# A hybrid decoder layer on one core: the two token mixers run half by half, 192 instead of 160 tokens take the gathered path, and the one-hots become float32

## The chip, the cores and the metric

The kernel runs on one core of a Trainium2 chip. TensorE multiplies matrices, VectorE (DVE in the profile) and ScalarE (ACT) work on tiles elementwise, GpSimd (POOL) here only issues the gathers of expert rows, and SyncE (SP) issues most of the other transfers. The metric is the device time of one execution in microseconds, lower being better. Before the change it is 3966.98 us, the median of three runs (3959.84 to 3968.33).

## What is computed

One decoder layer for 512 tokens of width 2048, with a final norm. Two mixers read the same normed input: HGRN2, a gated linear recurrence over chunks of 64 tokens with 8 heads, and latent attention (MLA) with 8 heads. Gates merge them, an output projection follows. Then comes PEER, a channel mixer in which each token picks 8 x 16 of 16384 single-neuron experts, and a gated per-layer embedding.

```python
proj = rms_norm(x, norm_mix) @ w_in
hq, hf, hi, hog, mq, mkv, mkr, ga, gb = split(proj)
o_a = hgrn2_branch(hq, hf, hi, hog, lb, hg_norm)      # S_t = diag(exp(g_t)) S_{t-1} + k_t v_t^T
o_b = mla_branch(mq, mkv, mkr, positions, ...)        # causal attention
y = sigmoid(ga) * (o_a @ w_a) + sigmoid(gb) * (o_b @ w_b)
x = x + y @ w_o
x = x + peer_ffn(rms_norm(x, norm_ffn), peer_wq, k1, k2, u, v)
x = x + sigmoid(rms_norm(x, norm_ple) @ w_pg) * (p @ w_pe)
return rms_norm(x, norm_final)
# peer_ffn, per token and head: q = h @ wq; top 16 of 128 keys in each half, top 16 of
# their 256 sums; gate = softmax; z = u[e] . h; out = sum(gate * gelu(z) * v[e])
```

## The kernel before

**Products.** A float32 product is made of three passes on values split in two: `hi` is the rounded value, `lo` the rest, and `mm3` (L151 to L153) adds `hi*hi`, `hi*lo` and `lo*hi`. Weights arrive in tiles of 128x2048 (1 MB) as two transfers into the ring `raw` (four halves); `Stream.split` makes `hi` on ScalarE (L115) and `lo` on VectorE (L116), into rings of four halves each. A tile is used in 48 matmuls, with all tokens of the stage as the moving columns (`cols_proj`) or with the weights as moving columns and blocks of 128 tokens as the fixed side (`rows_proj`, L181 to L183).

**Stages.** First the mixers for all 512 tokens: HGRN2 in two groups of four heads (projections, then per head exponentials, products, seven chunk states and the readout), then the latents, the rotary key and attention in four pairs of heads. Between the heads of attention run the gate projections of tokens 0 to 255 (`gate_proj`). Up to here, and for merge, output projection and PEER scores of tokens 0 to 255, the compiler's planner orders the instructions. Then `manual_schedule` begins: from here each engine works in the order in which the program is written. Tokens 256 to 511 go through their 32 gate projections, merge, output projection and scores. Then come U and V: in U (128 steps of 48 matmuls) every expert's `u` is multiplied with the tokens of the dense path, in V (128 steps of 48 matmuls) the activations are multiplied with every expert's `v`. A tail with the embedding gate and the output follows.

**Two paths of PEER.** The first NA + NX = 160 tokens don't take the dense path: their experts' rows are gathered. One gather brings 128 rows of 2048 values, one per partition; a `row_op` on VectorE multiplies it with `hrow` (u, L915) or adds it to `hrow` with a coefficient (v, L924), and calls the next gather (L904). Three row buffers are in flight. Tokens 0 to 127 need 128 gathers for u and 128 for v; the 32 tokens of NX lie four times side by side and need 32 and 32: 320 `row_op` in all. The other ND = 352 tokens are dense. For each, `gate_tokens` builds two one-hot tiles (L997 to L1003), multiplies them (L1008) so that its gates land on a 128x128 grid of experts, and stores that grid to DRAM (`G_s`), from which V reads it (`act_load`).

**Work beside.** `background()` runs once per weight tile in the manual part and takes topk (`prep_A` for tokens 0 to 127, `prep_B(b)` for block b) and `row_op` from the list `todo` by steps. In U, `work` holds `prep_B(2)`, `prep_B(3)` and `gate_tokens`, and `row_op` is spread evenly; in V too (VROWS = 148). Before U there are NEARLY = 36 `row_op`.

Of the kernel before, what the change touches and what calls it, by code (L numbers as in the profile page):

```python
# [20 lines left out]
T = 512  # L21
# [4 lines left out]
NX = 32  # L26
# [24 lines left out]
def kernel(ctx: ExitStack, tc: tile.TileContext, a, dbg=None):  # L51
# [44 lines left out]

    class Stream:
# [158 lines left out]
    def load_constants():  # L256
        m = t2()[:, :384]
        nc.sync.dma_start(m, a["masks"])
        nc.sync.dma_start(cst, a["consts"])
        V.tensor_copy(masks, m)  # L260
        V.tensor_copy(tril, m[:, 128:256])

# [13 lines left out]
    xpool = tc.alloc_tile_pool(name="xpool", bufs=1, side="right")  # L276
    xh = xpool.tile([128, KT, T], F32R, name="xh")
    xl = xpool.tile([128, KT, T], F32R, name="xl")

    def x_chunk(k):  # L280
        r = t2()
        nc.sync.dma_start(r, a["xT"][k])
        split(xh[:, k], xl[:, k], r, g_mix[:, k:k + 1])

    xblocks = [(xh[:, :, b * 128:(b + 1) * 128], xl[:, :, b * 128:(b + 1) * 128]) for b in range(4)]

    hg = tc.alloc_tile_pool(name="hg", bufs=1, side="left")
    masks = hg.tile([128, 384], F32R, name="masks")
    tril = hg.tile([128, 128], U32, name="tril")

    ss = tmp.tile([128, 4], F32, name="ss", bufs=1)
    ss2 = tmp.tile([128, 2, 4], F32, name="ss2", bufs=1)

# [11 lines left out]


# [15 lines left out]
    abuf = []  # L322
    for i in range(2):
        t = hg.tile([128, 4, 128], F32, name=f"abuf{i}")
        G.memset(t, 0.0)
        abuf.append(t)

    def first_chunks(i):
        x_chunk(2 * i)
        x_chunk(2 * i + 1)  # L330
        if i == 1:
            load_constants()

    rc_mix = rr_mix = None
    for hh in range(2):
        cs = slice(hh * 512, (hh + 1) * 512)
        ps_f = rows_proj([a["w_f"][hh, q] for q in range(4)], xblocks,
                         None if hh else first_chunks)
        if hh == 0:
            rc_mix, rr_mix = x_stats()  # L340
        lb, omlb = lower_bound(cs)
        gh = hg.tile([128, 4, 512], F32R, name="gh")
        gl = hg.tile([128, 4, 512], F32R, name="gl")
        k_t = hg.tile([128, 4, 512], F32, name="k_t")
        v_t = hg.tile([128, 4, 512], F32, name="v_t")
        qT = hg.tile([128, 4, T], F32, name="qT")
        ogT = hg.tile([128, 4, T], F32, name="ogT")
        for b in range(4):
            f = t2()
            S.activation(f, ps_f[b], AF.Sigmoid, scale=rc_mix[:, b:b + 1])  # L350
            V.tensor_tensor(f, f, omlb, op=OP.mult)
            V.tensor_tensor(f, f, lb, op=OP.add)
            V.tensor_scalar(k_t[:, b], f, -1.0, 1.0, op0=OP.mult, op1=OP.add)
            S.activation(f, f, AF.Ln)
            split(gh[:, b], gl[:, b], f)
            if hh == 0:
                dump(f"g_t{b}", f)
        ps_i = rows_proj([a["w_i"][hh, q] for q in range(4)], xblocks)
        for b in range(4):
            S.activation(v_t[:, b], ps_i[b], AF.Copy, scale=rc_mix[:, b:b + 1])  # L360
        for c in range(4):
            ps = cols_proj(a["w_q"][hh * 4 + c], xh, xl)
            V.tensor_tensor(qT[:, c], ps, rr_mix, op=OP.mult)
        for c in range(4):
            ps = cols_proj(a["w_og"][hh * 4 + c], xh, xl)
            V.tensor_tensor(ogT[:, c], ps, rr_mix, op=OP.mult)
            S.activation(ogT[:, c], ogT[:, c], AF.Silu)
        if hh == 0:
            dump("v_t", v_t)
            dump("qT", qT)  # L370
            dump("ogT", ogT)

        kTs = []
        for h in range(4):
            hs = slice(h * 128, (h + 1) * 128)
            kT_ps = mx()
            for b in range(4):
                TE.transpose(kT_ps[:, b * 128:(b + 1) * 128], k_t[:, b, hs], ident)
            kT = hg.tile([128, T], F32, name="kT", bufs=4)
            S.activation(kT, kT_ps, AF.Copy)  # L380
            kTs.append(kT)
        for b in range(4):
            dps = mx()
            TE.matmul(dps, lhsT=masks[:, 256:], rhs=gh[:, b], start=True, stop=False)
            TE.matmul(dps, lhsT=masks[:, 256:], rhs=gl[:, b], start=False, stop=True)
            e4 = t2()
            S.activation(e4, dps, AF.Exp)
            V.tensor_tensor(k_t[:, b], k_t[:, b], e4, op=OP.mult)

        for h in range(4):  # L390
            head = hh * 4 + h
            hs = slice(h * 128, (h + 1) * 128)
            e1 = hg.tile([128, 4, 128], F32, name="e1", bufs=2)
            e3 = hg.tile([128, 4, 128], F32, name="e3", bufs=1)
            qe = hg.tile([128, T], F32, name="qe", bufs=1)
            e2 = hg.tile([128, 4, 128], F32, name="e2", bufs=1)
            for bb in range(2):
                bps = mx().rearrange("p (b m t) -> p b m t", b=2, m=2)
                for b in range(2):
                    TE.matmul(bps[:, b], lhsT=gh[:, bb * 2 + b, hs], rhs=masks[:, :256], start=True, stop=False)  # L400
                    TE.matmul(bps[:, b], lhsT=gl[:, bb * 2 + b, hs], rhs=masks[:, :256], start=False, stop=True)
                o = slice(bb * 2, bb * 2 + 2)
                S.activation(e1[:, o], bps[:, :, 0], AF.Exp)
                S.activation(e2[:, o], bps[:, :, 0], AF.Exp, scale=-1.0)
                S.activation(e3[:, o], bps[:, :, 1], AF.Exp)
            qin, kin, eb = flat(e1), flat(e2), flat(e3)
            V.tensor_tensor(qin, qin, qT[:, h], op=OP.mult)
            V.tensor_tensor(kin, kin, kTs[h], op=OP.mult)
            V.tensor_tensor(qe, eb, qT[:, h], op=OP.mult)
            A_ps = mx()  # L410
            for b in range(4):
                bs = slice(b * 128, (b + 1) * 128)
                TE.matmul(A_ps[:, bs], lhsT=kin[:, bs], rhs=qin[:, bs], start=True, stop=True)
            ab = abuf[head % 2]
            for b in range(4):
                V.copy_predicated(ab[:, b], tril, A_ps[:, b * 128:(b + 1) * 128])
            states = [None]
            for n in range(7):
                dS = mx()
                r = slice((n % 2) * 64, (n % 2) * 64 + 64)  # L420
                TE.matmul(dS[:, :128], lhsT=k_t[r, n // 2, hs], rhs=v_t[r, n // 2, hs],
                          start=True, stop=True)
                st = hg.tile([128, 128], F32, name="st", bufs=8)
                if n == 0:
                    S.activation(st, dS[:, :128], AF.Copy)
                else:
                    V.scalar_tensor_tensor(st, states[-1], eb[:, n * 64 + 63:n * 64 + 64], dS[:, :128],
                                           op0=OP.mult, op1=OP.add)
                states.append(st)
            o_ps = mx()  # L430
            for b in range(4):
                bs = slice(b * 128, (b + 1) * 128)
                TE.matmul(o_ps[:, bs], lhsT=v_t[:, b, hs], rhs=ab[:, b], start=True, stop=False,
                          skip_group_check=True)
                for n in (2 * b, 2 * b + 1):
                    if n:
                        ns = slice(n * 64, n * 64 + 64)
                        TE.matmul(o_ps[:, ns], lhsT=states[n], rhs=qe[:, ns], start=False,
                                  stop=n == 2 * b + 1, skip_group_check=True)
# [6 lines left out]
        for h in range(4):  # L446
# [4 lines left out]
            dump(f"oa{head}", kTs[h])  # L451
    hg.release()

    def gate_proj(src, dst):
        w = Stream(src)
# [1060 lines left out]
```

## Time and profile before

| | |
|---|---|
| median of three runs | 3966.98 us |
| profiled execution, its own time | 3957.45 us |
| its span | 3955.7 us |
| TensorE busy | 3873.2 us, 98% |
| VectorE busy | 2950.8 us, 75% |
| ScalarE busy | 1750.3 us, 44% |
| GpSimd busy | 496.4 us, 13% |
| moved | 1011.64 MB, mean 256 GB/s |
| granted TensorE clock, mean share | 0.993 |

Busy time says how long an engine had an instruction in it. Matmuls are pipelined, so the time that one costs is the distance from its start to the next one's start, which is shorter than its own duration. The stages by time from the start of the span: mixers and gates of tokens 0 to 255 until 889.4 us, merge to scores of tokens 0 to 255 until 1178.1, gates of tokens 256 to 511 until 1375.1, their merge to scores until 1725.8, U until 2764.6, V until 3758.5, tail until 3955.7.

### The profile page before, as it was taken

The numbers are of one execution on the slowest core, as the hardware profiler recorded it, in microseconds if no ns is written. First come the engines' busy times: TensorE is split into PE (matmuls) and PEld (weight loads), VectorE is DVE, ScalarE is ACT, GpSimd is POOL, SyncE is SP. The second block draws the span as 40 slices with busy tenths as digits, with TensorE's granted clock in tenths as the row PEclk, the third lists the DMA queues.
The fourth block names the chain that finished last, engine by engine and source line by source line (L and its number), as shares of the span: only waits on it lengthen the run. The fifth ranks groups of instructions, "written<-read, shape, count | busy, mean of one in ns | idle before, by whom it ended". The sixth has DMA issues, their size and how long they took to land. (4 is left out here: it accounts for less than half of the span.)

```text
span 3955.7 us, 63576 instructions
## 1 busy us (share of the span) xinstructions
PE 3873.2 (98%) x24825; PEld 3677.9 (93%) x24825; DVE 2950.8 (75%) x4439; ACT 1750.3 (44%) x2814; POOL 496.4 (13%) x326
## 2 busy tenths in 40 slices
PE   9999999999999999899999999999999999999998
PEld 7878788899999989899999999999999999999987
DVE  5252555557658798789989898886888989899854
ACT  5242434345544434455555466663333333333443
POOL 0000000000000111012222222221122222222000
PEclk9999999999999999999999999999999999999999
DMA  5222234457766988788888888989999999899533
GB/s 212 96 75 96 70 99 134 130 184 238 231 203 205 330 280 299 268 293 314 317 319 301 306 324 308 338 310 357 359 346 346 368 356 353 330 360 361 195 120 99
DMA packets 312875, 1011.64 MB, mean 256 GB/s; under 512 B 29952, under 2 KB 127744, under 8 KB 269696
## 3 DMA queue, kind: packets, MB, share of 16 engines
q1 hardware_dynamic: 224032, 595.02, 44.1%
q0 software_dynamic: 46080, 335.56, 22.3%
q10 hardware_dynamic: 42464, 77.00, 5.1%
q8 instruction: 196, 3.21, 0.3%
q14 instruction: 103, 0.84, 0.1%
HBM read 931.18 MB, written 76.28 MB: 255 GB/s over the span
## 5 line engine op out<-in xcount | busy, mean ns | idle before, releaser
L116 DVE TENSOR_TENSOR lo<-raw,hi 128x1024 fp32r<-128x1024 f32 x966 | 1163.7, 1221 | 599.2 <-ACT hi L115 590.7
L115 ACT ACTIVATE hi<-raw 128x1024 fp32r<-128x1024 f32 x966 | 1012.5, 1056 | 1222.1 <-PE acc L152 819.1
L153 PE MATMUL acc<-hBh,lo 128*128 128x352 f32 x2048 | 662.1, 323 | 0.0
L152 PE MATMUL acc<-hBl,hi 128*128 128x352 f32 x2048 | 661.0, 323 | 0.0
L151 PE MATMUL acc<-hBh,hi 128*128 128x352 f32 x2048 | 658.7, 322 | 0.0
L904 POOL DMA_INDIRECT row<-in_peer_u_dram,eA x128 | 206.5, 1613 | 2194.2 <-PE acc L153 1298.8
L153 PEld LDWEIGHTS acc<-hBh,lo 128*128 128x128 f32 x2048 | 385.5, 188 | 0.0
L151 PEld LDWEIGHTS acc<-hBh,hi 128*128 128x128 f32 x2048 | 385.3, 188 | 0.0
L152 PEld LDWEIGHTS acc<-hBl,hi 128*128 128x128 f32 x2048 | 384.9, 188 | 0.0
L153 PE MATMUL acc<-ahx,lo 128*128 128x352 f32 x1024 | 331.5, 324 | 2.0 <-DVE lo L116 1.9
L151 PE MATMUL acc<-ahx,hi 128*128 128x352 f32 x1024 | 329.9, 322 | 1.1 <-DVE x L1237 1.1
L153 PE MATMUL acc<-ah,lo 128*128 128x352 f32 x1024 | 330.4, 323 | 0.5 <-DVE lo L116 0.5
L151 PE MATMUL acc<-ah,hi 128*128 128x352 f32 x1024 | 330.9, 323 | 0.0
L152 PE MATMUL acc<-alx,hi 128*128 128x352 f32 x1024 | 330.4, 323 | 0.0
L152 PE MATMUL acc<-al,hi 128*128 128x352 f32 x1024 | 329.0, 321 | 0.0
L151 PE MATMUL acc<-xh,hi 128*128 128x256 f32 (+1 forms) x912 | 305.1, 335 | 0.0
L153 PE MATMUL acc<-xh,lo 128*128 128x256 f32 (+1 forms) x912 | 305.0, 334 | 0.0
L152 PE MATMUL acc<-xl,hi 128*128 128x256 f32 (+1 forms) x912 | 304.2, 334 | 0.0
L924 DVE SCALAR_TENSOR_TENSOR hrow<-row,zA,hrow 128x2048 f32<-128x2048 f32 x127 | 297.9, 2345 | 0.8
L915 DVE SCALAR_TENSOR_TENSOR row<-row,hrow 128x2048 f32<-128x2048 f32 x128 | 291.6, 2281 | 6.8 <-DMA row<-in_peer_u_dram,eA 6.8
L904 POOL DMA_INDIRECT row<-in_peer_v_dram,eA x128 | 188.2, 1470 | 645.3 <-DVE hrow L924 610.5
L153 PEld LDWEIGHTS acc<-ahx,lo 128*128 128x128 f32 x1024 | 192.6, 188 | 3.7 <-DVE lo L116 3.7
(434 smaller groups left out, 8430.7 us busy)
## 6 DMA issues: line engine op xcount, KB each, us to landing
raw<-in_uT_dram SPq DMA_DIRECT2D x256, 512.0 KB, 7.5
raw<-in_vB_dram SPq DMA_DIRECT2D x256, 512.0 KB, 8.4
raw<-in_w_ga_dram SPq DMA_DIRECT2D x64, 512.0 KB, 4.2
raw<-in_w_gb_dram SPq DMA_DIRECT2D x64, 512.0 KB, 4.7
raw<-in_w_o_dram SPq DMA_DIRECT2D x64, 512.0 KB, 4.9
raw<-in_wq_dram SPq DMA_DIRECT2D x64, 512.0 KB, 4.7
z_s<-t ACTq DMA_DIRECT2D x128, 176.0 KB, 6.7
G_s<-stage ACTq DMA_DIRECT2D x11, 2048.0 KB, 15.0
```

Of the source, the lines that this page charges most:

```text
L115: S.activation(hi, raw, AF.Copy)
L116: V.tensor_tensor(lo, raw, hi.bitcast(F32), op=OP.subtract)
L151: TE.matmul(out, lhsT=lh, rhs=rh, start=start, stop=False)
L152: TE.matmul(out, lhsT=lh, rhs=rl, start=False, stop=False)
L153: TE.matmul(out, lhsT=ll, rhs=rh, start=False, stop=stop)
L904: G.indirect_dma_start(out=row, out_offset=None, in_=a["peer_v" if v else "peer_u"], in_offset=bass.IndirectOffsetOnAxis(ap=e[:, s:s + 1], ...
L915: V.scalar_tensor_tensor(row, row, 1.0, hrowX if x else hrow, op0=OP.mult, op1=OP.mult, accum_out=(zX if x else zA)[:, s:s + 1])
L924: V.scalar_tensor_tensor(o, row, c[:, s:s + 1], o, op0=OP.mult, op1=OP.add)
```

## The change

The mixers become functions of a half, `hgrn(hf, ...)` and `attention(hf, ...)`. They run for tokens 0 to 255 at the start and for tokens 256 to 511 where the gates of that half stood, now in the part that the planner orders, with all of the half's 32 gate projections between the heads. `cols_proj` therefore has 256 moving columns, and each mixer weight is loaded and split twice. The second half takes the HGRN2 states, keys, values and the rotary key of the first from DRAM (`hgs_s`, `kn_s`, `vv_s`, `kr_s`). Each `Stream` of the second mixers calls `background()`, so topk and `row_op` run beside them. NX goes from 32 to 64, so ND from 352 to 320, and there are 384 `row_op`: NEARLY = 90, VROWS = 146, the rest in U. One-hots are float32: the right one carries the gate itself in 128 columns, where there were two halves of it in 256, and the sum of the halves from PSUM (L1014) goes. `manual_schedule` now begins at the merge of tokens 256 to 511.

```diff
-NX = 32
+NX = 64
         def __init__(self, src, now=True, before=None):
+            if now and running[0]:
+                background()
...
     def cols_proj(src, xh, xl, kt=KT):
         w = Stream(src)
-        ps = acc()
+        ps = acc()[:, :xh.shape[-1]]
...
+    def scaled_cols(out, ps, hf):
+        if hf:
+            S.activation(out, ps, AF.Copy)
+        else:
+            V.tensor_tensor(out, ps, rr_mix[:, :H], op=OP.mult)
...
+    def hgrn(hf, xh, xl, before):
...
+                states = [None]
+                if hf:
+                    states[0] = hg.tile([128, 128], F32, name="st", bufs=8)
+                    nc.sync.dma_start(states[0], hgs_s[head])
+                for n in range(3 if hf else 4):
...
+                if not hf:
+                    nc.sync.dma_start(hgs_s[head], states[4])
...
+    def attention(hf, xh, xl):
...
+            if hf:
+                nc.sync.dma_start(vv[:, :2], vv_s[hp])
+                for c in range(2):
+                    t = t2()[:, :H]
+                    nc.sync.dma_start(t, kn_s[hp * 2 + c])
+                    split(kn[c][0][:, :H], kn[c][1][:, :H], t)
...
+                fill_in(3, hf, xh, xl)
...
-                        if not hf:
-                            S.activation(g, g, AF.Sigmoid)
+                        S.activation(g, g, AF.Sigmoid)
...
-            l = upool.tile([128, 128], F32R, name="ohl", bufs=8)
-            r = upool.tile([128, 2, 128], F32R, name="ohr", bufs=8)
-            i1T, i2T = (slots[b][:, n, t:t + 1] for n in range(2))
+            l = upool.tile([128, 128], F32, name="ohl", bufs=8)
+            r = upool.tile([128, 128], F32, name="ohr", bufs=8)
+            i1T, i2T, gT = (slots[b][:, n, t:t + 1] for n in range(3))
             S.activation(l, iota, AF.Abs, scale=-1.0, bias=i1T)
-            V.scalar_tensor_tensor(r, iota[:, None, :].to_broadcast([128, 2, 128]), i2T,
-                                   slots[b][:, 2:4, t:t + 1].to_broadcast([128, 2, 128]),
-                                   op0=OP.is_equal, op1=OP.mult)
+            V.tensor_scalar(r, iota, i2T, gT, op0=OP.is_equal, op1=OP.mult)
...
-                TE.matmul(ps[:, i * 256:i * 256 + 256], lhsT=l, rhs=flat(r), start=True, stop=True)
+                TE.matmul(ps[:, i * 128:i * 128 + 128], lhsT=l, rhs=r, start=True, stop=True)
...
-                S.activation(st[:, :, o:o + 4], hi, AF.Copy)
-                V.tensor_tensor(st[:, :, o:o + 4], st[:, :, o:o + 4], lo, op=OP.add)
+                S.activation(st[:, :, o:o + 4], ps.rearrange("p (t j) -> p j t", t=4), AF.Copy)
...
-    VROWS = 148
-    NEARLY = 36
-    todo = phase(20, prep_A()) + phase(60, merge(prep_B(1), [(2.5, row_op)] * NEARLY))
+    NEARLY = 90
+    part = 24
+    todo = (phase(18, prep_A()) + phase(40, merge(prep_B(1), [(2.5, row_op)] * part))
+            + phase(70, [(2.5, row_op)] * (NEARLY - part)))
...
+    running[0] = True
+    hgrn(1, xBh, xBl, None)
+    attention(1, xBh, xBl)
...
+    running[0] = False
...
+    ordered = tc.manual_schedule()
+    ordered.__enter__()
+    manual[0] = True
+    VROWS = 146
```

## Rows read from the trace of the kernel before

**Rows 1.** Page, part 1: engine, busy us, share, instructions.

```profile
PE 3873.2 (98%) x24825; PEld 3677.9 (93%) x24825; DVE 2950.8 (75%) x4439; ACT 1750.3 (44%) x2814; POOL 496.4 (13%) x326
```

**Rows 2.** Windows by stage; columns end with granted clock, DMA share, GB/s.

```profile
0.00:889.40 889.40, 879.04 (x4886) 740.25 (x4887) 431.08 (x698) 364.57 (x543) 1.19 (x6) 1.00 0.37 122
889.40:1178.10 288.70, 284.91 (x2405) 279.33 (x2404) 187.03 (x273) 154.50 (x238) 0.00 (x0) 1.00 0.71 225
1178.10:1375.10 197.00, 185.71 (x1543) 184.90 (x1542) 157.99 (x390) 85.89 (x114) 13.62 (x10) 0.97 0.75 259
1375.10:1725.80 350.70, 318.17 (x2472) 306.65 (x2470) 289.40 (x508) 151.64 (x223) 39.04 (x29) 0.96 0.83 284
1725.80:2764.60 1038.80, 1034.19 (x6509) 1029.02 (x6508) 911.83 (x1440) 581.08 (x1198) 229.58 (x136) 1.00 0.87 318
2764.60:3758.50 993.90, 990.37 (x6177) 987.02 (x6176) 875.62 (x969) 339.77 (x406) 212.99 (x145) 1.00 0.90 338
```

**Rows 3.** Waits in V (2764.6 to 3758.5): us in total, times, longest.

```profile
DVE lo L116 <- ACT hi L115: 68.7, 66, 3.2
DVE zt L1172 <- DMA gt<-G_s: 41.1, 14, 5.0
```

**Rows 4.** Timeline of PE: first and last of three unbroken series, 256, 352, 512 columns.

```profile
1200.70 0.28 PE L151 MATMUL acc<-xBh,hi 128*128 128x256 f32 x1
...
1206.71 0.28 PE L151 MATMUL acc<-xBh,hi 128*128 128x256 f32 x1
3000.13 0.32 PE L153 MATMUL acc<-ahx,lo 128*128 128x352 f32 x1
...
3006.84 0.32 PE L153 MATMUL acc<-ahx,lo 128*128 128x352 f32 x1
3845.88 0.39 PE L153 MATMUL acc<-x2h,lo 128*128 128x512 f32 x1
...
3852.68 0.39 PE L153 MATMUL acc<-x2h,lo 128*128 128x512 f32 x1
```

**Rows 5.** Lines of PE by form: 512-column matmuls with x in the mixers, one of three passes.

```profile
L151 PE MATMUL acc<-xh,hi 128*128 128x512 f32 x400 | 158.8, 397 | 0.0
```

**Rows 6.** Timeline of PE: float32 matmuls of 128 columns, and the next instruction.

```profile
838.46 1.16 PE L605 MATMUL mx<-t,vv 128*128 128x128 f32 x8
839.37 0.36 PE L151 MATMUL acc<-xh,hi 128*128 128x256 f32 x1
```

**Rows 7.** Lines of VectorE in U (1725.8 to 2764.6): rows and one-hots.

```profile
L915 DVE SCALAR_TENSOR_TENSOR row<-row,hrow 128x2048 f32<-128x2048 f32 x92 | 209.4, 2280 | 0.0
L998 DVE SCALAR_TENSOR_TENSOR ohr<-cst,slots 128x256 fp32r<-128x256 f32 x352 | 145.7, 477 | 0.1
L1014 DVE TENSOR_TENSOR stage<-stage,wide 128x512 f32<-128x512 f32 x88 | 59.1, 683 | 5.8 <-ACT stage L1013 1.5
```

**Rows 8.** Lines of VectorE in V: one addition of a product to `x2`.

```profile
L1237 DVE TENSOR_TENSOR x<-x,acc 128x352 f32<-128x352 f32 x255 | 130.6, 512 | 3.4 <-DMA x<-x1s 3.4
```

**Rows 9.** Lines of VectorE, 0 to 889.4, then three of 1178.1 to 1375.1.

```profile
L116 DVE TENSOR_TENSOR lo<-raw,hi 128x1024 fp32r<-128x1024 f32 x165 | 201.7, 1224 | 256.8 <-ACT hi L115 254.3 <-DMA gb<-t 1.6 <-DMA raw<-in_w_gb_dram 0.6
L116 DVE TENSOR_TENSOR lo<-raw,hi 128x1024 fp32r<-128x1024 f32 x63 | 75.1, 1216 | 19.3 <-ACT hi L115 19.2
L915 DVE SCALAR_TENSOR_TENSOR row<-row,hrow 128x2048 f32<-128x2048 f32 x8 | 18.3, 2284 | 6.8 <-DMA row<-in_peer_u_dram,eA 6.8
L159 DVE TENSOR_TENSOR olB<-t,ohB 128x256 fp32r<-128x256 f32 x13 | 5.4, 417 | 1.3 <-ACT ohB L158 1.3
```

**Rows 10.** Windows in V: its main stretch, and the 40 us with most bytes.

```profile
2764.60:3690.00 925.40, 921.87 (x5740) 918.69 (x5739) 818.48 (x865) 306.14 (x363) 212.99 (x145) 1.00 0.94 352
3046.00:3086.00 40.00, 40.00 (x254) 40.00 (x252) 38.74 (x41) 13.22 (x17) 10.27 (x7) 1.00 1.02 391
```

**Rows 11.** DMA issues: name, engine, count, us to landing; one POOL line in U.

```profile
row<-in_peer_u_dram,eA POOLq DMA_INDIRECT x128, 9.2
L904 POOL DMA_INDIRECT row<-in_peer_u_dram,eA x89 | 153.8, 1728 | 523.2 <-DVE row L915 512.1 <-DVE lo L116 9.2 <-issue 1.8
```

More of the change, by code (lines that the diff above doesn't have):

```diff
@@ L273 @@
     G_s = dram.tile([ND // TC, 128, 128 * TC], F32, name="G_s")
[L276 to L289, printed above, removed]
+    hgs_s = [dram.tile([128, 128], F32, name=f"hgs{i}") for i in range(8)]
+    kn_s = [dram.tile([128, H], F32, name=f"kns{i}") for i in range(8)]
+    vv_s = [dram.tile([128, 2, 256], F32, name=f"vvs{i}") for i in range(4)]
+    kr_s = dram.tile([128, H], F32, name="krs")
     ss = tmp.tile([128, 4], F32, name="ss", bufs=1)
     ss2 = tmp.tile([128, 2, 4], F32, name="ss2", bufs=1)
+    rc_mix = rr_mix = None
     def x_stats():
@@ L320, in lower_bound @@
         return e0, e1
[L322 to L355, printed above, removed]
-            if hh == 0:
[L357 to L397, printed above, removed]
@@ L405 @@
[L405 to L413, printed above, removed]
@@ L414 @@
[L414 to L439, printed above, removed]
@@ L440 @@
-            S.activation(kTs[h], o_ps, AF.Square)
-            V.scalar_tensor_tensor(ogT[:, h], o_ps, g_hg[:, head:head + 1], ogT[:, h], op0=OP.mult, op1=OP.mult)
-        for h in range(4):
-            ms = mx()
-            TE.matmul(ms, lhsT=ones, rhs=kTs[h], start=True, stop=True)
-            S.activation(kTs[h], ms, AF.Ln, scale=1.0 / 128, bias=eps)
-        for h in range(4):
-            head = hh * 4 + h
-            S.activation(kTs[h], kTs[h], AF.Exp, scale=-0.5)
-            V.tensor_tensor(kTs[h], kTs[h], ogT[:, h], op=OP.mult)
-            nc.sync.dma_start(oa_s[head], kTs[h])
-            dump(f"oa{head}", kTs[h])
@@ new lines, in hgrn @@
+                V.tensor_tensor(kin, kin, kTs[h], op=OP.mult)
+                V.tensor_tensor(qe, eb, qT[:, h], op=OP.mult)
+                A_ps = mx()[:, :H]
+                for b in range(2):
+                    bs = slice(b * 128, (b + 1) * 128)
+                    TE.matmul(A_ps[:, bs], lhsT=kin[:, bs], rhs=qin[:, bs], start=True, stop=True)
+                ab = abuf[head % 2]
+                for b in range(2):
+                    V.copy_predicated(ab[:, b], tril, A_ps[:, b * 128:(b + 1) * 128])
@@ new lines, in hgrn @@
+                if not hf:
+                    nc.sync.dma_start(hgs_s[head], states[4])
+                o_ps = mx()[:, :H]
+                for b in range(2):
+                    bs = slice(b * 128, (b + 1) * 128)
+                    TE.matmul(o_ps[:, bs], lhsT=v_t[:, b, hs], rhs=ab[:, b], start=True, stop=False,
+                              skip_group_check=True)
+                    for n in (2 * b, 2 * b + 1):
+                        if states[n] is not None:
+                            ns = slice(n * 64, n * 64 + 64)
+                            TE.matmul(o_ps[:, ns], lhsT=states[n], rhs=qe[:, ns], start=False,
+                                      stop=n == 2 * b + 1, skip_group_check=True)
@@ new lines, in hgrn @@
+                S.activation(kTs[h], o_ps, AF.Square)
+                V.scalar_tensor_tensor(ogT[:, h], o_ps, g_hg[:, head:head + 1], ogT[:, h], op0=OP.mult, op1=OP.mult)
+            for h in range(4):
+                ms = mx()[:, :H]
+                TE.matmul(ms, lhsT=ones, rhs=kTs[h], start=True, stop=True)
+                S.activation(kTs[h], ms, AF.Ln, scale=1.0 / 128, bias=eps)
+            for h in range(4):
+                head = hh * 4 + h
+                S.activation(kTs[h], kTs[h], AF.Exp, scale=-0.5)
+                V.tensor_tensor(kTs[h], kTs[h], ogT[:, h], op=OP.mult)
+                nc.sync.dma_start(oa_s[head][:, hf * H:hf * H + H], kTs[h])
@@ new lines, in x_pool, with first_chunks @@
+    def x_pool(hf):
+        pool = tc.alloc_tile_pool(name=f"xpool{hf}", bufs=1, side="right")
+        return pool, pool.tile([128, KT, H], F32R, name=f"xh{hf}"), pool.tile([128, KT, H], F32R, name=f"xl{hf}")
+    xpool, xh, xl = x_pool(0)
+    def first_chunks(i):
+        for k in (2 * i, 2 * i + 1):
+            r = t2()[:, :H]
+            nc.sync.dma_start(r, a["xT"][k][:, :H])
+            split(xh[:, k], xl[:, k], r, g_mix[:, k:k + 1])
+    hgrn(0, xh, xl, first_chunks)
+    attention(0, xh, xl)
@@ L773 @@
     ypool.release()
[L774 to L776 removed]
+    xB, xBh, xBl = x_pool(1)
     rcA = []
@@ L1063 @@
     ol = opool.tile([128, 16, H], F32R, name="olB")
-    mix = []
-    for n, (src, dst) in enumerate((("w_ga", ga_s[1]), ("w_gb", gb_s[1]))):
-        for i in range(16):
-            w = block(a[src][i])
-            ps = acc()[:, :H]
-            for k in range(KT):
-                mm3(ps, *w.part(k, KT), xBh[:, k], xBl[:, k], k == 0, k == KT - 1)
-            def gate(i=i, ps=ps, dst=dst):
-                t = t2()[:, :H]
-                S.activation(t, ps, AF.Sigmoid)
-                nc.scalar.dma_start(dst[i], t)
-            late.append(gate)
-            after_products()
-            if len(mix) > 1:
-                late.append(mix.pop(0))
-            if n and i or not n and i == 15:
-                mix.append(mixed(n * i, 1, oh, ol))
-    late.extend(mix)
-    run_late()
+    for i in range(16):
+        mixed(i, 1, oh, ol)()
+        if gates_todo:
+            fill_in(1, 1, xBh, xBl)
+    assert not gates_todo
+    running[0] = False
     xB.release()
```

428 lines of the change are left out of this document (251 added, 177 removed).

## The prediction, made before the changed kernel ran

> **What bounds the kernel now.** I read the page's busy shares first: TensorE has an instruction in it for 98% of the span [rows 1], so the first question is what its matmuls cost, not which engine waits. Second the windows by stage [rows 2]: is TensorE full in each, and how full is VectorE, which makes every `lo` half? In the mixers (0 to 889.4) TensorE is busy 879.0 us and VectorE 431.1, under half. From 1178 on the picture turns. In the gates of tokens 256 to 511 VectorE is busy 158.0 of 197.0, in their merge to scores 289.4 of 350.7, in U 911.8 of 1038.8, in V 875.6 of 993.9. Third the timeline, for what one matmul costs [rows 4]: 51 distances in 6.01 us make 117.8 ns at 256 columns, 42 in 6.71 us make 159.8 ns at 352, 30 in 6.80 us make 226.7 ns at 512.
>
> With these prices the stages show what TensorE loses. U and V are 128 x 48 = 6144 dense matmuls each, 981.8 us. V lasts 993.9, so it loses 12. U also has 352 one-hot matmuls of 256 columns (41.5 us) and loses 15.5. The gate stage is 32 x 48 matmuls of 256 columns, 180.9 us, and lasts 197.0: 16 lost. Merge to scores takes 288.7 us for tokens 0 to 255; for the other half it also holds 96 matmuls of 512 columns for `w_pe` (21.8 us) and takes 350.7, so 40 are lost there. The granted clock of 0.97 and 0.96 in these two says that part of them ran at the lower of its two levels. The kernel is bound by TensorE with VectorE close behind, closest in the second half, V and U.
>
> **Dense columns, 352 to 320.** The line through 256 and 352 columns gives 145.8 ns at 320; taking off 32 columns at the price between 352 and 512 (0.418 ns each) gives 146.4. I take 146.0: 6144 x 13.8 ns = 85 us off in each of U and V (82 to 86). The matmul count stays.
>
> **One-hots.** 352 f32r matmuls of 256 columns (41.5 us) become 320 float32 ones of 128. Four of those stand in the timeline as eight records from 838.46 to 839.37, so 228 ns each [rows 6]: 73 us, plus 31 (26 to 36). On VectorE, L1014 (59.1 us) goes and L998 (477 ns each) works on half the width: no dearer than now, so 60 to 130 us less. Against that stand 148 instead of 136 `row_op` in U at 2.3 us [rows 7], plus 28. VectorE in U falls to some 820 of 985 us, its share from 88% to 83%, and I keep the loss of 15 (within 15 either way). **U: 1038.8 - 85 + 31 = 985.**
>
> **V.** TensorE alone would need 993.9 - 85 = 909. VectorE is the question. It has two `row_op` less (5 us), and some 495 additions, products and splits whose width falls by 32. A 256-wide operation takes 417 ns and a 352-wide one 512 [rows 8, 9], so 32 columns are 32 ns and all of it 16 us: 875.6 becomes 855. It also waits 68.7 us for ScalarE's `hi` and 41.1 us for `gt`, the gates' transfer from DRAM [rows 3]. The first is mostly slack, VectorE being ahead; the second is a landing time, which doesn't shrink with the steps, and splits queue behind the waiting product. With no wait left VectorE needs 855, less than TensorE; with all of both, 965 to 973. I take the 41 whole and half of the 69: **V: 930**, 909 to 973, so 64 saved of 85. VectorE replaces TensorE as what is late next.
>
> Transfers: the main stretch moves 352 GB/s x 925.4 us = 326 MB at a DMA share of 0.94 [rows 10]. Less two rows (1 MB each) and 60 transfers smaller by 64 KB, 320 MB remain; in 866 us that is 369 GB/s. The best 40 us moved 391 with TensorE full [rows 10], so the engines can do it, with 6% to spare. The Trainium skill, "DMA: Bandwidth & Descriptors", section Specifications, gives about 358 GB/s as the limit of HBM for one core. The 391 GB/s here go past it, so I don't use it; by it the 320 MB would take an estimated 894 us, V 958, and the sum would be 28 us longer.
>
> **Mixers in halves, TensorE.** Matmuls with 512 moving columns become two of 256: 1200 with `xh` (400 in each of three passes) [rows 5] and 288 of the latents (four pairs of heads, six products, 12 each). Each pair costs 235.6 instead of 226.7 ns, plus 13 us. `rows_proj` keeps its matmuls, two blocks twice. Mixers with both sets of gates are now 889.4 + 197.0 = 1086.4; without the 16 lost, and with the 13, 1083.6. Attention gives the second half more, so about 530 to 540 and 545 to 555.
>
> **First half.** 81 weight tiles where the whole mixers had 81 for twice the tokens; one per about 5.7 us of TensorE. VectorE's own work outside splits is 431.1 - 201.7 = 229 us [rows 2, 9], some 13 of it the gates, so at most 133 per half with its fixed parts; with 81 x 2.44 us of splits and the gates, 344 of 540. That cover is ample. The start is tighter: `x` (4 MB for the statistics) and eight weight tiles must land within about 44 us instead of 88. I take 10 lost, 0 to 20.
>
> **Second half.** VectorE here: 162 splits x 1.19 us = 193; own work 120 (the multiplications by `rr_mix` go to ScalarE); two topk; 46 `row_op`. The steps are `background()` calls, one per tile: 81 of them take 18 + 40 steps with 24 `row_op` and 23 of the last 70 steps, so 22 more: 46 x 2.36 = 109. One topk comes from the gate stage: 158.0 less 75.1 of splits, 18.9 of eight `row_op` with their accumulator reads, 5.4 of `olB` [rows 9] leaves 58.6, of which some 9 belong to the next block: 49. Sum 193 + 120 + 98 + 109 = 520 of 550, 94%. What that costs TensorE the trace shows at two ends: U and V, at 89% of their ideal time, lose 1.2 to 1.5%; merge to scores, 289 of an ideal 310 or 93%, loses 13%. So 8 to 72 us of 550. I take 42, the middle, since the planner's order is unlike both. New waits: `hgs_s`, `kn_s`, `vv_s` and `kr_s` were stored more than 300 us earlier, but their loads stand on SP's queue between weight loads, and a store there waits for its producer while weight loads queue behind it. In the old mixers such stores (`oa_s`, `ob_s`) stood on SP as well and TensorE stayed at 99% [rows 2], so nothing more for that.
>
> **Merge to scores, tokens 256 to 511.** 44 `row_op` instead of 29 (+35 us of VectorE), most of a topk less (-40), the sigmoid of the gates now on ScalarE here, and the manual order starts here with empty rings. No change, within 15. Tail: none; its `row_op` are over and it works on all 512 tokens.
>
> **Sum**, against the profiled execution of 3957.45 us (span 3955.7): mixers and gates 1083.6 + 10 + 42 = 1136, plus 49; U -54; V -64; rest 0: -69, so 3888. The median of the runs shown is 9.5 us above the profiled execution; put on that, **3898 us**, faster by 1.7%. All good ends together make about 3800, all bad ones 4030. Some 0.2%, 8 us, is what a measurement of this kernel can tell from no change.
>
> **Rivals.**
>
> *All of it hides.* The splits stay ahead in the second mixers as in U, and V's waits shrink with its steps: mixers 1084 + 8, V 915, U 975. For it: 40 us of V with VectorE at 38.7 and TensorE full [rows 10]. Against: that lasts 40 us, here it would have to hold 850. Sum 3957 + 6 - 64 - 79, on the median's scale about 3830 (3800 to 3855). Chance 0.20.
>
> *Slower: the planner packs `row_op` closer than three buffers can feed.* Beside the second mixers the order is the planner's, and it may move `row_op` forward into any free time of VectorE. A gather lands 9.2 us after its issue, which takes GpSimd 1.7 [rows 11], and with the 2.3 of the `row_op` a buffer turns in 13.2: three feed one per 4.4 us. Packed at VectorE's own pace each waits 2 us, and every weight split queued behind it on VectorE waits too: 46 x 2 = 92 us. With no slack on VectorE that goes to TensorE, on top of the 72 of the bad end: mixers 1256 instead of 1136, total about 4018 (3980 to 4060). It decides from about 1.5 us lost per `row_op`. For it: in the gate stage TensorE lost 16 us with only eight `row_op`. Against: evenly spread, one comes each 12 us, and in U and V VectorE hardly waits for gathers. Chance 0.16.
>
> *V gets nothing.* Both of VectorE's waits stay whole and the transfers take the best slices' pace at most: V 973, the second mixers at their bad end: 3898 + 43 + 30 = 3971 (3955 to 3985), no change that can be told. Chance 0.08.
>
> *Columns aren't the price.* If 320 columns cost what 352 do, U and V keep 170 us: 4045 or more. The three widths lie on one line [rows 4], so 0.03.
>
> **Chances and range.** Forecast 0.53 (3855 to 3955), the others as above. Faster by over 0.2%: 0.53 + 0.20 and a small part of the third, 0.75. Within 0.2%: 0.06. Slower: 0.19. From 3825 to 3990 leaves out a part of the first rival and most of the two slow ones, about 0.2.
>
> **What would show it.** Distance between dense matmuls 146 ns; float32 one-hots about 228 ns. U 970 to 1000, V 909 to 973, and in V VectorE over 90% busy with waits for `gt` as long as now. First mixers with gates near 545; the second 560 to 620 with VectorE over 85% busy and TensorE waiting for `lo`; merge to scores near 350. Wrong if the second mixers pass 640 (then: waits of `row_op` for rows), if V stays above 980, or if the planner lets TensorE idle at the changes from HGRN2 to attention, which shorter halves cover less.

## The result and the profile after

The changed kernel takes 3982.9 us, the median of six runs (3979.6 to 3989.3), against 3963.3 for the kernel before beside it (six runs, 3958.6 to 3968.3): a ratio of 1.0053, 95% interval 1.0043 to 1.0063. It is slower by 0.5%, where 1.7% faster was forecast. The time lies inside the range of 3825 to 3990, near its slow end, and on the other side of no change.

Page, part 1, of the changed kernel, to be held against [rows 1]: engine, busy us, share of the span (3983.2 us), instructions.

```profile
PE 3775.5 (95%) x26621; PEld 3637.3 (91%) x26621; DVE 3088.6 (78%) x4670; ACT 1880.6 (47%) x3024; POOL 586.0 (15%) x392
```

TensorE has 98 us less to do than in [rows 1] and the span is 27 us longer: about 125 us more in which it stands idle. Where they lie is read from the windows by stage, as [rows 2]: stretch, length, then busy us of PE, PEld, DVE, ACT and POOL, granted clock, DMA share, GB/s. In order: first mixers with gates, merge to scores of tokens 0 to 255, second mixers with gates, merge to scores of tokens 256 to 511, U, V, tail.

```profile
0.00:564.40 564.40, 535.32 (x3918) 498.32 (x3919) 336.54 (x554) 298.36 (x442) 0.76 (x6) 0.99 0.62 189
564.40:852.90 288.50, 285.59 (x2406) 280.23 (x2405) 185.81 (x273) 154.91 (x236) 0.00 (x0) 1.00 0.74 224
852.90:1508.10 655.20, 561.56 (x4020) 518.08 (x4019) 507.87 (x1037) 308.59 (x472) 65.81 (x51) 0.92 0.68 229
1508.10:1857.60 349.50, 316.35 (x2468) 303.66 (x2467) 280.47 (x369) 161.47 (x253) 61.28 (x44) 0.97 0.93 333
1857.60:2850.30 992.70, 982.20 (x6798) 980.25 (x6797) 825.49 (x1303) 552.83 (x1121) 256.96 (x148) 0.99 0.91 339
2850.30:3785.30 935.00, 913.69 (x6176) 906.04 (x6175) 854.41 (x971) 331.61 (x408) 201.16 (x143) 1.00 0.93 353
3785.30:3983.20 197.90, 180.83 (x849) 150.73 (x847) 98.02 (x165) 72.85 (x94) 0.00 (x0) 0.96 0.35 109
```

| stage, us | before | predicted | after |
|---|---|---|---|
| first mixers with gates | 889.4 (whole) | 545 | 564.4 |
| merge to scores, 0 to 255 | 288.7 | 289 | 288.5 |
| second mixers with gates | 197.0 (gates only) | 591 | 655.2 |
| merge to scores, 256 to 511 | 350.7 | 351 | 349.5 |
| U | 1038.8 | 985 | 992.7 |
| V | 993.9 | 930 | 935.0 |
| tail | 197.2 | 197 | 197.9 |

U and V gave 105 of the 118 us forecast. The mixers and gates came to 1219.6 instead of 1136, and 64 of those 84 us lie in the second mixers. There TensorE is busy for 561.6 of 655.2 us, at a mean granted clock of 0.92, while VectorE, forecast with 520 us of work, has 507.9: its work is as forecast, yet it is idle for 147 us, and TensorE waits all the same. The next views tell why. (The stages miss by 95 us in sum, the medians by 85: the forecast put the median 9.5 us above the profiled execution, and it came out 2 below.)

Waits in that stage (852.9 to 1508.1): engine and line, whom it waited for, us in total, times, longest.

```profile
PE acc L155 <- DVE t L510: 24.2, 1, 24.2
PE mx L607 <- DVE t L603: 12.0, 8, 5.2
PE acc L186 <- DVE lo L120: 11.9, 4, 10.7
...
DVE row L932 <- DMA row<-in_peer_u_dram,eA: 7.4, 7, 3.8
```

TensorE is idle for 93.6 us of the stage, and 84 of these end with VectorE, only 13 of them with the half of a weight (`lo`). The longest wait is for L510, which multiplies for the rotary key and stands at the end of a chain of short operations. VectorE's timeline through that chain (start us, duration, line, operation, tiles, and idle time before it in brackets):

```profile
1193.69 0.35 DVE L488 TENSOR_SCALAR t<-t,cst 128x256 f32<-128x256 f32 x1
1193.96 2.28 DVE L932 SCALAR_TENSOR_TENSOR row<-row,hrow 128x2048 f32<-128x2048 f32 x1
1196.17 0.07 DVE L932 DVE_READ_ACCUMULATOR row<-row,hrow 128x1 f32 x1
1196.17 0.28 DVE L489 TENSOR_SCALAR t<-t 128x256 f32<-128x256 f32 x1
...
1197.22 2.28 DVE L932 SCALAR_TENSOR_TENSOR row<-row,hrow 128x2048 f32<-128x2048 f32 x1
1199.43 0.08 DVE L932 DVE_READ_ACCUMULATOR row<-row,hrow 128x1 f32 x1
1199.43 0.88 DVE L492 SCALAR_TENSOR_TENSOR t<-t,t 128x256 f32<-128x256 f32 x2
1201.21 2.29 DVE L932 SCALAR_TENSOR_TENSOR row<-row,hrow 128x2048 f32<-128x2048 f32 x1 [0.91 <-DMA row<-in_peer_u_dram,eA]
...
1204.10 2.28 DVE L932 SCALAR_TENSOR_TENSOR row<-row,hrow 128x2048 f32<-128x2048 f32 x1
...
1207.78 0.74 DVE L847 MAX8 cv<-t 128x8 f32<-128x256 f32 x2
...
1212.22 0.43 DVE L510 TENSOR_TENSOR t<-acc,sinT 64x256 f32<-64x256 f32 x1
```

The links take 0.28 to 0.43 us each. Between them stand four `row_op` (L932) of 2.28 and, before L510, 4.4 us of topk (L847 and its neighbours). From L487 at 1193.4 to the end of L510 the chain takes 19.3 us, some 5 of them its own. VectorE works its instructions in one order, and a link whose data is ready waits behind a row that nobody is waiting for. The Trainium skill, "PSUM — Partial Sum Buffer", section Engine vs sequencer instructions, says the same of its queue ("strict FIFO"); this timeline agrees.

Windows of the changed kernel: 40 us around that chain, and the stage's last 155 us.

```profile
1173.00:1213.00 40.00, 9.95 (x75) 8.89 (x75) 33.86 (x65) 6.34 (x10) 11.12 (x9) 0.63 0.90 316
1353.00:1508.10 155.10, 154.59 (x1253) 147.70 (x1253) 83.43 (x123) 75.46 (x121) 0.00 (x0) 1.00 0.61 183
```

In the first TensorE is busy for a quarter of the time and VectorE for 85%; the granted clock falls to 0.63, so much of this stretch ran at the lower of the two levels (1.2 of 2.4 GHz). In the last 155 us GpSimd issues no gather, VectorE is half idle and TensorE full. The rows that the program spreads from the 18th weight tile to the last were all done before: 25 before the chain begins at 1193.4, 4 within it, 17 by 1353. Kept at their places in the program, 12 would stand before the chain (an experiment below). So the planner did move rows forward: all 46 stand between 992 and 1342, ahead of the 155 us in which TensorE hardly waits.

### The profile page after: what moved, and what is told of

The parts are those of the page before. It is cut to its first block, busy times and chain, and to the rows that moved or that the text cites. A ratio compares the mean times of both kernels' runs of the same rounds, so it can differ in the third digit from the quotient of the medians.

```text
span 3983.2 us, 68241 instructions
## 1 busy us (share of the span) xinstructions
PE 3775.5 (95%) x26621; PEld 3637.3 (91%) x26621; DVE 3088.6 (78%) x4670; ACT 1880.6 (47%) x3024; POOL 586.0 (15%) x392
## 5 line engine op out<-in xcount | busy, mean ns | idle before, releaser
L155 PE MATMUL acc<-hBh,hi 128*128 128x320 f32 x2048 | 641.0, 313 | 1.6 <-ACT hi L119 1.6
L157 PE MATMUL acc<-hBh,lo 128*128 128x320 f32 x2048 | 634.3, 310 | 0.7 <-DVE lo L120 0.7
L156 PE MATMUL acc<-hBl,hi 128*128 128x320 f32 x2048 | 634.3, 310 | 0.0
L155 PE MATMUL acc<-xh,hi 128*128 128x256 f32 x1824 | 515.8, 283 | 0.0
L157 PE MATMUL acc<-xh,lo 128*128 128x256 f32 x1824 | 513.8, 282 | 1.4 <-DVE lo L120 1.4
L156 PE MATMUL acc<-xl,hi 128*128 128x256 f32 x1824 | 513.9, 282 | 0.0
L155 PEld LDWEIGHTS acc<-xh,hi 128*128 128x128 f32 x1824 | 345.1, 189 | 4.7 <-issue 2.4
L157 PEld LDWEIGHTS acc<-xh,lo 128*128 128x128 f32 x1824 | 345.2, 189 | 3.4 <-DVE lo L120 1.8
L156 PEld LDWEIGHTS acc<-xl,hi 128*128 128x128 f32 x1824 | 346.2, 190 | 0.8 <-issue 0.6
L155 PE MATMUL acc<-ahx,hi 128*128 128x320 f32 x1024 | 317.6, 310 | 4.3 <-DVE x L1241 2.1
```

What stands on the lines that cost most here:

```text
L155: TE.matmul(out, lhsT=lh, rhs=rh, start=start, stop=False)
L156: TE.matmul(out, lhsT=lh, rhs=rl, start=False, stop=False)
L157: TE.matmul(out, lhsT=ll, rhs=rh, start=False, stop=stop)
```

## The experiments

All kernels below are the changed one with a further edit, except the last three, which are the kernel before with a part of the change. Theory at the outset: the second mixers lose by what runs beside them on VectorE. Rivals: rows that wait for their gathers, states and keys that come late from DRAM, and the halving itself.

**No work beside the second mixers.** Rows and topk wait for the merge behind them, their steps (not shown) drawn together to fit its 50 weight tiles.

```diff
-    running[0] = True
+    running[0] = False
     hgrn(1, xBh, xBl, None)
```

> The changed kernel, but nothing runs beside the second mixers: both topk and all 90 rows before U wait for the 50 weight tiles from merge to scores. Nothing is left out. Read is the second mixers' stage alone (655 us in the changed kernel, ideal 550), not the total, since merge to scores gets about 200 us more of VectorE. Theory A (VectorE's work beside, put between the links of short dependent chains, makes the matmuls wait): the stage falls to 560-590 us, near the first mixers' 564. Rival B (the halves themselves lose it: shorter covers, loads of states and keys on SP's queue, whatever runs beside): it stays at 630 or more. In between, both.

One execution took 4143.8 us, since the stage behind is now overloaded (611 us). The window of the second mixers alone:

```profile
852.20:1402.50 550.30, 536.82 (x4019) 499.26 (x4018) 311.84 (x477) 302.89 (x464) 0.56 (x2) 0.99 0.57 175
```

550.3 us, in the middle of the 545 to 555 worked out as the ideal, and less than the 560 to 590 expected. States, keys and values still come from DRAM here, and TensorE waits 0.3 us for them; of 655.2 us, 105 are due to the work beside. First and second half together are 1114.5 us (564.2 and 550.3); the whole mixers with gates were 1086.4, with rows and topk beside the last 197 of them, so halving by itself costs at least 28.

**Topk beside, rows moved to U.** The 90 early rows shrink to the 44 that fit behind the second mixers.

```diff
-    NEARLY = 90
-    part = 24
+    NEARLY = 44
...
+    todo = (phase(18, prep_A()) + phase(40, prep_B(1)) + [(24, lambda: None)]
+            + phase(46, [(2.5, row_op)] * NEARLY))
```

> The changed kernel, with both topk still beside the second mixers, but none of the 46 rows: 44 rows stay in merge to scores and 46 more are done in U (194 there instead of 148). If rows are what breaks the chains (theory A, rows): second mixers 590-615 us. If topk does (A, topk): 630 or more. Rival B: 640 or more. U gets 46 x 2.36 = 109 us more of VectorE, from 825 to about 934 of 993 us: if it is bound by TensorE it grows by 0 to 15 us, if VectorE's share counts as in V, by 25 to 50. Total 3930-3960 by A with U holding, about 3985-4000 by B.

3986.7 us, ratio to the kernel before 1.0059 (1.0037 to 1.0080), the same as with the rows. Windows of the second mixers and of U:

```profile
851.80:1445.00 593.20, 552.30 (x4022) 512.10 (x4021) 412.54 (x946) 306.84 (x470) 3.90 (x5) 0.96 0.55 171
1796.40:2849.90 1053.50, 1001.67 (x6797) 996.02 (x6796) 923.95 (x1397) 555.02 (x1122) 367.59 (x194) 0.97 0.95 366
```

So the 46 rows cost 62 us in the second mixers and the two topk 43. In U the same 46 rows cost 61, where 50 at most were expected, though VectorE there is busy for 88% only; the transfers run at a DMA share of 0.95. The rows are a burden in either place, 1.3 us of time for each.

**Rows pinned.** A `row_op` outside the manual part keeps its place in the program.

```diff
-            V.scalar_tensor_tensor(row, row, 1.0, hrowX if x else hrow, op0=OP.mult, op1=OP.mult,
-                                   accum_out=(zX if x else zA)[:, s:s + 1])
+            ins = V.scalar_tensor_tensor(row, row, 1.0, hrowX if x else hrow, op0=OP.mult, op1=OP.mult,
+                                         accum_out=(zX if x else zA)[:, s:s + 1])
+            if not manual[0]:
+                tc.keep_in_program_order(ins)
```

> The changed kernel, each row operation of the part that the planner orders pinned behind what the program names before it on VectorE, so the planner can't move it forward. 12 instead of 25 rows then stand before the rotary chain of the second half and none between its links. Theory A with the planner's moving forward as its cause: second mixers 600-630 us, total 3930-3960. If the amount of VectorE's work counts and not its place: 645-660, total 3975-3985.

3965.5 us, ratio 1.0003 (0.9993 to 1.0012): 17 us less than the change as it was. Its window of the second mixers, the 40 us that were worst before, and the rotary chain in its timeline:

```profile
854.00:1481.60 627.60, 566.19 (x4023) 521.52 (x4022) 503.95 (x1034) 303.45 (x468) 63.59 (x50) 0.94 0.68 233
1173.00:1213.00 40.00, 28.42 (x191) 25.95 (x190) 34.41 (x78) 16.60 (x29) 3.62 (x3) 0.83 0.50 173
```

```profile
1175.50 0.29 DVE L487 CAST t<-t 128x256 f32<-128x256 int32 x1 [2.06 <-DMA t<-in_pos_dram]
1175.83 0.35 DVE L488 TENSOR_SCALAR t<-t,cst 128x256 f32<-128x256 f32 x1
...
1176.87 1.80 DVE L492 SCALAR_TENSOR_TENSOR t<-t,t 128x256 f32<-128x256 f32 x4
...
1185.11 0.43 DVE L510 TENSOR_TENSOR t<-acc,sinT 64x256 f32<-64x256 f32 x1
```

No row stands between the links now, and the chain takes 10.0 us instead of 19.3; 12 rows come before it instead of 25. VectorE has nearly the same work (503.9 against 507.9 us; one row has slipped into the next stage) and the stage is 28 us shorter. That is place, not amount. Of the 28 the next stage gives back 12: merge to scores takes 361.9 us instead of 349.5, so the total stays above the 3930 to 3960 expected.

**All of the work beside pinned**, topk too: every VectorE operation issued by `background()` in that stage keeps its place.

```diff
+            def call(*args, **kw):
+                ins = f(*args, **kw)
+                return tc.keep_in_program_order(ins) if beside[0] else ins
...
+            beside[0] = running[0]
             f()
+            beside[0] = False
```

> The changed kernel with every VectorE instruction of the work beside the second mixers pinned behind what the program names before it, the topk as well as the rows (rows alone: second mixers 628 us instead of 655, total 3966). If the place between the links counts for topk too: 600-620 us, total 3940-3960. If the amount counts from here on: 625-632, total within 5 of 3966.

3960.3 us, ratio 0.9990 (0.9981 to 1.0000); the second mixers:

```profile
852.40:1481.50 629.10, 558.29 (x4022) 516.91 (x4021) 502.77 (x1032) 304.24 (x469) 68.86 (x49) 0.94 0.68 233
```

Pinning topk as well brings nothing more in this stage: TensorE's longest waits are now for `lo`, 33.3 us in six waits, where they were 12.1 with the rows alone pinned. Where the program puts the steps is no better for topk than where the planner does. The 5 us between the two totals lie within their intervals.

**Topk only at the gate tiles.** Rows as in the kernel with rows moved to U; topk steps run, pinned, at the 32 tiles of the gate projections alone. Their matmuls wait for no chain, and they stand between and behind the heads of attention: HGRN2, the latents and the rotary key stay free of topk, which begins at 1146 us.

```diff
+            running[0] = bool(hf)
...
+            running[0] = False
...
+    todo = phase(11, prep_A()) + phase(21, prep_B(1)) + phase(47, [(2.5, row_op)] * NEARLY)
```

> As the run with 46 rows moved to U (both topk beside the second mixers, no rows; second mixers 593 us, where without work beside them they took 550), but the topk steps run only at the 32 gate tiles, whose matmuls wait for no chain, pinned there on VectorE. The amount of VectorE's work in the stage is the same. If the place beside the chains costs: second mixers 555-575 us. If the amount costs: 585-600. U stays at about 1053; total 3945-3970 in the first case, about 3985 in the second.

3961.2 us, ratio 0.9998 (0.9988 to 1.0008); the second mixers:

```profile
854.20:1423.60 569.40, 541.62 (x4019) 502.79 (x4018) 406.44 (x935) 300.25 (x463) 3.72 (x5) 0.98 0.57 178
```

569.4 against 593.2 us with the same topk (VectorE 406 and 412 us): 24 of topk's 43 us were place too.

**Half of the statistics later.** The first mixers also missed their time. Here the squares of `x` for tokens 256 to 511 move behind the first HGRN2.

```diff
+                    x_squares((0, 1))
+                    rc_mix, rr_mix = x_stats(0)
...
+        if hf == 0:
+            x_squares((2, 3))
+            rr_B.append(x_stats(1)[1])
```

> The changed kernel, with the squares of x for tokens 256 to 511 (2 MB, four activations) done behind the first HGRN2 instead of before the first gate. In the changed kernel TensorE is busy 42 of the first 60 us. If the bytes of x at the start cost that: first mixers 564 to about 557 us, total -7. If the first 60 us hang on other loads or on the chain of the statistics: within 2 us.

3998.5 us, ratio 1.0090 (1.0073 to 1.0107), worse than the change itself; its first mixers take 571.5 us instead of 564.4. Windows of this kernel, at the start and where the squares now stand, then the same two of the changed kernel:

```profile
30.00:40.00 10.00, 7.24 (x23) 4.80 (x22) 5.21 (x13) 7.85 (x11) 0.00 (x0) 0.83 0.89 320
180.00:240.00 60.00, 54.04 (x430) 53.02 (x429) 28.70 (x44) 32.06 (x44) 0.00 (x0) 0.94 0.60 191
```

```profile
30.00:40.00 10.00, 2.95 (x13) 2.05 (x11) 0.33 (x2) 6.78 (x11) 0.00 (x0) 0.84 0.85 279
180.00:240.00 60.00, 59.78 (x492) 58.27 (x490) 32.15 (x45) 30.20 (x43) 0.00 (x0) 1.00 0.58 177
```

The bytes at the start do cost: TensorE gains 4 us in those ten. At their new place it loses 6, and 5.8 of these are one wait, for the copy of `kT` on ScalarE, which stands there behind the squares and a weight's `hi` that waited 2.3 us for its bytes. That the bytes of `x`, which come through the ring of the weights, were moved and not saved is my reading. The profiled execution is 12 us above the median of its four, so a part of the 7 us that the first mixers are longer may be its own, and its later stages aren't read.

**One-hots alone**, on the kernel before: float32, 128 columns, as in the diff of the change.

> The kernel before with float32 one-hots alone, 160 tokens on gathered rows. TensorE in U gets 352 x 0.11 us = 39 us more, VectorE about 110 less. If U is bound by TensorE: U 1039 to 1070-1080, total +30 to +40. If VectorE's place in U is worth half its time, as the run with 46 rows more in U says (61 us for 109): U 1010-1030, total -10 to -30.

3987.9 us, ratio 1.0066 (1.0050 to 1.0083). U:

```profile
1729.40:2795.60 1066.20, 1063.80 (x6860) 1063.33 (x6860) 812.17 (x1350) 585.26 (x1197) 198.05 (x137) 1.00 0.85 310
```

**192 tokens on rows alone**, on the kernel before.

```diff
-NX = 32
+NX = 64
...
-    VROWS = 148
+    VROWS = 146
```

> The kernel before with one part alone: 192 tokens on gathered rows (VROWS = 146, so 202 rows in U), mixers whole, one-hots as before. VectorE in U: 912 - 19 for 32 one-hots less + 66 x 2.36 = about 1049 us, TensorE 897 + 38 = 935. Bound by VectorE: U 1065-1095, V 935, total 3930-3955. If VectorE were no bound there: U 950-960, total about 3820.

3985.5 us, ratio 1.0061 (1.0043 to 1.0079). U, and TensorE's two longest waits for VectorE there:

```profile
1724.30:2845.70 1121.40, 1029.33 (x6478) 992.93 (x6477) 1032.54 (x1497) 556.69 (x1125) 407.34 (x203) 0.95 0.92 352
```

```profile
PE wide L1008 <- DVE ohr L998: 58.0, 26, 9.1
...
PE acc L153 <- DVE lo L116: 18.8, 12, 4.5
```

U was expected at 1065 to 1095 if VectorE bound it, and the total at 3930 to 3955: both came out longer. ScalarE also waits 222 us there for weights from DRAM, against 42 in the kernel before, so the transfers may have a share in it.

**Both, with the mixers whole.** The two edits above together.

> The kernel before with two of the change's three parts: 192 tokens on gathered rows (VROWS = 146, 36 rows before U, so 202 in U) and float32 one-hots. The mixers stay whole. If the halves are what loses the gain: stages as in the kernel before up to U (1726 us), U 1055-1075 (the run with 194 rows in U took 1053), V 935, total 3915-3940, faster than both kernels. If the rest loses it: 3965 or more.

3917.4 us (3915.0 to 3925.8), ratio 0.9885 (0.9869 to 0.9902): faster than both kernels by more than 1%. U:

```profile
1724.30:2786.90 1062.60, 1005.38 (x6797) 996.62 (x6796) 942.48 (x1414) 555.75 (x1123) 370.67 (x203) 0.98 0.96 371
```

The parts don't add. Alone the one-hots cost 24 us, since U with 136 rows is TensorE's (1063.8 of 1066.2 us busy) and their matmuls are dearer. Alone the 64 more `row_op` cost 22: V falls to 939.0 us, but U becomes VectorE's (1032.5 of 1121.4) and grows by 83. Together they gain 46, because the one-hots take 90 us from VectorE in the very stage where the rows need them, and, as I read it, their dearer matmuls fall into time that TensorE loses anyway. ScalarE's waits for weights are the same in both kernels with 202 rows in U (222 and 220 us) while U falls by 59, which speaks for VectorE and against the transfers in these 59.

This kernel also prices the halves. Mixers and gates take 890.1 + 194.3 = 1084.4 us here and 1219.6 in the changed kernel, 135 more. The halves let 54 more rows run before U, and U is 70 shorter (992.7 instead of 1062.6). That leaves 65; V and merge to scores are some 6 shorter too, and the profiled executions differ by 59, the medians by 3982.9 - 3917.4 = 65.5.

## Why the prediction was wrong, step by step

**Second mixers: the failed step.** "I take 42, the middle, since the planner's order is unlike both": the loss was 105 (655.2 against 550.3). The counts were right: 46 rows, 507.9 us of VectorE against 520. What failed was to price VectorE by its share. In U, V and merge to scores, from which the ends of 8 and 72 came, much of VectorE's work is weight splits that run ahead of their use, so, as I read it, a row of 2.3 us is paid out of that lead as long as there is one. In the mixers TensorE follows chains of short operations, each link waiting for the last, and there is no lead to pay from. The stage with chains and rows side by side had no row in the trace of before; the mixers there ran without rows [rows 2], at 99%. The bound from both sides should have had an end worked out from the chains: 46 rows and two topk all in chains are 109 + 98 = 207 us of time, and half of that came.

**The clock: a term put at nothing.** Of the 105, 80 are idle time of TensorE (93.6 against 13.5 us). The other 25 are busy time: 4020 matmuls keep it busy for 561.6 us at a granted clock of 0.92, 4019 without work beside for 536.8 at 0.99. The forecast had no term for this, though it had read 0.97 and 0.96 in two stages with rows.

**How the 105 divides.** Rows 62, topk 43. Pinning the rows gives 28 back, putting topk at the gate tiles 24. What stays, some 50 us, is open: the amount of the work, or places that weren't tried. The sum of both cures in one kernel was not run.

**The rival "slower".** Its first half came true: the planner does pack rows forward. Its price did not. It had each row wait 2 us for its gather, 92 in all, with the splits behind; rows waited 7.4 us in all, 4.7 of them at the rotary key. The row's own 2.3 us behind which a link stands was the price. "Wrong if the second mixers pass 640 (then: waits of `row_op` for rows)" named the right figure and the wrong wait. Nor did TensorE wait mainly for `lo`, as the forecast said (11.9 us).

**First mixers.** 564.4 instead of 545. The start is as forecast: in the first 60 us TensorE is busy 42.2 us against 51.6 in the kernel before, so 9.4 are lost where 10 were put down. Not forecast were three stretches of short chains. A window of the kernel before, then four of the changed one:

```profile
0.00:60.00 60.00, 51.57 (x210) 40.68 (x211) 29.83 (x47) 39.32 (x54) 1.19 (x6) 1.00 0.78 287
```

```profile
0.00:60.00 60.00, 42.16 (x155) 31.67 (x156) 33.58 (x55) 40.00 (x58) 0.76 (x6) 0.91 0.80 266
120.00:180.00 60.00, 56.76 (x286) 45.48 (x285) 41.12 (x71) 38.96 (x58) 0.00 (x0) 1.00 0.44 138
240.00:300.00 60.00, 57.22 (x460) 54.81 (x459) 38.09 (x79) 37.74 (x60) 0.00 (x0) 1.00 0.48 144
300.00:360.00 60.00, 55.90 (x433) 53.47 (x433) 38.32 (x76) 28.16 (x46) 0.00 (x0) 0.97 0.57 168
```

The last three lose 10.1 us where the whole mixers lost 2 behind their start; TensorE's waits there are mostly for links of chains (3.8 us for L514, 1.6 for L402). The forecast named shorter halves that cover less, but only as a mishap without a price. My reading, which no run isolates: with half the columns the matmuls beside a chain cover half the time, while its links shrink by less (VectorE takes 0.68 us for 512 columns of float32 in this kernel and 0.42 for 256). The other 10 us of the difference are not loss. TensorE is busy 535.3 us here and 536.8 in the second mixers without work beside, 1072.1 in all; the forecast's 1083.6, less the 10.4 that TensorE was idle in the whole mixers, is 1073. So the work was right and its division was not: the 535 for the first half had to hold that idle start too, and 549 went to the second. That the second came to 550.3 without work beside, 13.5 of it idle, is in part luck.

**V: right, with two waits off against each other.** 935.0 against 930. Its waits and lines, as [rows 3] and [rows 8]:

```profile
DVE lo L120 <- ACT hi L119: 39.8, 36, 2.5
DVE zt L1176 <- DMA gt<-G_s: 31.6, 9, 4.3
```

```profile
L1241 DVE TENSOR_TENSOR x<-x,acc 128x320 f32<-128x320 f32 x255 | 122.1, 479 | 3.3 <-DMA x<-x1s 3.3
```

An addition takes 479 ns instead of 512, 33 less where 32 were put down; VectorE has 854.4 us, forecast 855. The waits are 71 us, taken as 75, but not as divided: that for `gt`, kept whole at 41, fell to 31.6, and that for `hi`, put at half of 69, is 39.8. VectorE did replace TensorE as what is late next: of TensorE's 21 us of idle time in V, 19 end with VectorE.

**U: right, with terms off against each other.** 992.7 against 985. Timeline of PE: first and last of 83 unbroken distances, four one-hot matmuls as eight records, and the line of their right half on VectorE:

```profile
3399.69 0.31 PE L156 MATMUL acc<-alx,hi 128*128 128x320 f32 x1
...
3411.86 0.31 PE L155 MATMUL acc<-ahx,hi 128*128 128x320 f32 x1
...
1886.33 1.05 PE L1025 MATMUL wide<-ohr,ohl 128*128 128x128 f32 x8
1887.13 0.39 PE L155 MATMUL acc<-hBh,hi 128*128 128x320 f32 x1
```

```profile
L1017 DVE TENSOR_SCALAR ohr<-cst,slots 128x128 f32<-128x128 f32 x320 | 88.1, 343 | 0.0
```

12.17 us for 83 distances are 146.6 ns, forecast 146.0; "columns aren't the price" is out. A one-hot matmul costs 0.80 / 4 = 200 ns, not 228, so 64 us instead of 73. (With one-hots alone, 352 of them lengthen U by 27.4 us: 78 ns each above the 118 of the old ones, so 196.) TensorE alone would need 6144 x 146.6 ns + 64 = 965, 5 less than forecast; the loss was 28 instead of 15. TensorE waits 7.3 us there for one-hots; what the other few are was not followed up.

**Transfers.** From 2850.3 to 3711.0 V moved 368 GB/s at a DMA share of 0.96; 369 was worked out. The figure of 358 from the Trainium skill was rightly left aside. The Trainium skill, "HBM Reference", section Specifications (TRN2), says that a core streaming alone goes above that share, which these 368 GB/s and the 371 over 1062.6 us of U in the kernel with whole mixers agree with.

**What was not weighed.** No step of the prediction asked what the halves alone bring and cost. With more rows done before it, U is 70 us shorter; against the 49 forecast for the mixers that would have left 20 us, and against the 135 measured the halves are the part to leave out.

## What to carry to other kernels

Work put beside a stage is priced by what it stands between: beside streams that run ahead it costs little until the engine is nearly full, and a piece that lands between two links of a chain of short dependent operations costs its own duration, however idle the engine is on average. Where a planner may move such work, look for its operations between the links of chains in the timeline, and pin it or give it to the tiles that have no chain. Of a change in several parts, work out each part with and without the others: here two that lose alone gain together, and a third takes the gain away.

## What the runs showed of the hardware that was not expected

The granted clock follows these gaps: the second mixers have a mean of 0.92, with 0.63 in the 40 us where TensorE was busy for 9.95, and 0.99 without work beside. After the wait of 24.2 us at the rotary key 18 matmuls of 256 columns, from 1213.79 to 1217.41, start 213 ns apart, against 117.8 in [rows 4]; so an idle TensorE is paid for beyond its idle time. A float32 matmul of 128 columns takes 200 ns between dense matmuls, against the 228 read from [rows 6]. And U with 194 rows is 61 us longer than with 148, though VectorE is busy for 88% and TensorE for 95% of it; transfers at a DMA share of 0.95 are the nearest suspect. VectorE waits 51 us there for gathered rows (2 with 148) and ScalarE 153 for weights (64), but no run tells them apart from VectorE's own work.
